# Moving the start addresses of matmul operands in on-chip memory: pads in three pools, wider MLP activation buffers, a smaller reserved scratch

## The chip, the cores and the metric

The kernel runs on one core of one Trainium2 chip. The metric is the device time of one execution in microseconds (us); the median of several runs counts. A core has five engines that work side by side and meet at semaphores: TensorE (PE) multiplies matrices, with its weight loads shown apart as PEld; VectorE (DVE) and ScalarE (ACT) do elementwise work and read PE's results out of PSUM, its accumulator memory; GpSimd (POOL) helps; SyncE (SP) issues most of the DMA transfers. All operands lie in SBUF, the on-chip memory, which has 128 partitions; a tile takes the same byte range in every partition, and an address here is a byte offset within a partition.

## The reference, cut to what matters

Two transformer-like blocks over 256 tokens of width 1024, all in float32. First two layers (a convolution mixed with attention, then a gated linear recurrence), each with a squared-ReLU MLP; then a block with two kinds of attention over 256 tokens and 256 context tokens.

```
h = rmsnorm(x, mix_norm[layer]); x = x + mixer(h)
x = x + square(relu(rmsnorm(x, mlp_norm[layer]) @ w_up)) @ w_down    # 1024 -> 4096 -> 1024
...
return second_block(rmsnorm(x, final_norm), ...)
```

Nearly all arithmetic is in products of activations with weight matrices.

## The kernel before, in words

Activations lie with the channel on the partition: a tile `[128, 8, 256]` holds 8 blocks of 128 channels by 256 tokens. A product in float32 accuracy is made from three products of a cheaper kind, on operands cut in a high and a low part of type float32r: `mm3` (lines 344 to 346) issues weights-high by x-high, weights-high by x-low, weights-low by x-high, all into one PSUM bank. One such matmul holds a 128 by 128 weight block (512 bytes in each partition) in the array and moves 256 tokens through (1,024 bytes in each partition). So each of the three has its own weight load, and the moving operand changes each time too. Products that give a value with the token on the partition (`vproj`, `v`) have it the other way round: the activations are held and 512 columns of a weight tile move.

Weights stream in as 243 units of 512 KB. `fetch` (line 289) issues the DMA of a unit into one of four buffers `raw`; `prep` makes `wh` by a copy (line 296, ACT; line 298 on DVE in some) and `wl` by a subtraction (line 299, DVE or POOL), each in a ring of six tiles of 4,096 bytes. `gemm` uses a unit as 8 weight blocks for one output block, `krow` as 8 output blocks for one row block. In `mlp`, an up pair takes two units (48 matmuls on `xsh` and `xsl`, the two parts of the normalised x, into the bank `mm`), and two units of the down product follow (48 matmuls on `mah` and `mal`, the two parts of the squared ReLU, into four banks `acc`), 16 times over. In each `mah` and `mal` tile there are two row blocks, so a matmul moves one half of it. The instruction stream of an engine runs in its order; that order is made when the program is built, by a scheduler that works from estimated durations, so that an added instruction on one engine can change the order on others.

Tile pools give out addresses in the order in which tiles are first asked for, after a block of 16,384 bytes that is reserved for descriptors of DMAs issued by POOL (there are none here). `wp` holds `raw`, `wh`, `wl`; `cp` holds constants, `xsh`, `xsl`, and the context's `hch`, `hcl` (these two later serve as `q8` and `oa`); phase pools (`l0`, `m0`, `l1`, `m1`, `b2`, ...) are stacked behind them and are given back at the end of their phase.

Of the kernel before, what the change touches and what calls it, by code (L numbers as in the profile page):

```python
# [11 lines left out]
F32 = mybir.dt.float32  # L12
F32R = mybir.dt.float32r
# [231 lines left out]
class Kern:  # L245
# [14 lines left out]
    def t(self, pool, shape, tag, dt=F32, bufs=1):  # L260
        self.n += 1
        return pool.tile(list(shape), dt, tag=tag, name=f"{tag}_{self.n}", bufs=bufs)

    def ps(self, tag="mm", cols=512):
        self.n += 1
        return self.psum.tile([128, cols], F32, tag=tag, name=f"{tag}_{self.n}", bufs=4)
# [32 lines left out]
        (nc.vector if lo == "v" else nc.gpsimd).tensor_tensor(wl, r, wh.bitcast(F32), op=ALU.subtract)  # L299

    def ready(self):
        """splits the next unit into its two parts"""
        i = self.u
        name = self.names[i]
        r = self.fetch(name)
        wh = self.t(self.wp, [128, 1024], "wh", F32R, bufs=RING)
        wl = self.t(self.wp, [128, 1024], "wl", F32R, bufs=RING)
        if i == 0:
            for q in range(4):
                for k in (2 * q, 2 * q + 1):  # L310
                    self.split_scaled(self.x[:, k], self.p("mix", k), self.xs[0][:, k], self.xs[1][:, k])
                if q % 2 == 0:
                    c = slice(q * 256, q * 256 + 512)
                    self.prep(r[:, c], wh[:, c], wl[:, c], "a", "v")
        elif i == 1:
            for c in (slice(0, 512), slice(512, 1024)):
                self.prep(r[:, c], wh[:, c], wl[:, c], "a", "v")
        else:
            c = POLICY.get(name, ("av",))
            c = c[self.cnt.get(name, 0) % len(c)]  # L320
            self.prep(r, wh, wl, c[0], c[1])
        self.cnt[name] = self.cnt.get(name, 0) + 1
        self.q.append((name, (wh, wl)))
# [34 lines left out]
        return ps  # L358

    def gfirst(self, name, x, mid=None):  # L360
        """two pairs at the start of a phase, the blocks of x that come last as late as the order allows"""
        ps, ws = [self.ps(), self.ps()], [[], []]
        for a, k0, k1 in ((0, 0, GA), (1, 0, GB), (0, GA, 8), (1, GB, 8)):
            if not ws[a]:
                ws[a] = [self.unit(name) for _ in range(2)]
            for k in range(k0, k1):
                c = slice(k * 128, k * 128 + 128)
                for i, w in enumerate(ws[a]):
                    self.mm3(ps[a][:, i * T:(i + 1) * T], (w[0][:, c], w[1][:, c]), (x[0][:, k], x[1][:, k]),
                             k == 0 and i == 0, k == 7)  # L370
            if k1 == 8 and mid:
                mid()
                mid = None
        return ps
# [45 lines left out]
        return r  # L420

    def across(self, rc, nt=2):
        """the tokens' values, a token a partition, to all partitions, a token a column"""
        ps = self.ps()
        for j in range(nt):
            self.lasts = self.nc.tensor.matmul(ps[:, j * 128:(j + 1) * 128], rc[:, j:j + 1].to_broadcast([128, 128]),
                                               self.ident, start=True, stop=True)
        return ps[:, :nt * 128]
# [12 lines left out]
    def run(self):  # L441
        nc, ctx = self.nc, self.ctx
        V, S, G, PE = nc.vector, nc.scalar, nc.gpsimd, nc.tensor
        self.wp = ctx.enter_context(self.pool("wp"))
        self.cp = ctx.enter_context(self.pool("cp"))
        self.dp = ctx.enter_context(self.pool("dp", bass.MemoryType.DRAM))
        self.psum = ctx.enter_context(self.pool("psp", bass.MemoryType.PSUM))
# [6 lines left out]
        with self.pool("xp") as xp:  # L454
# [6 lines left out]
            G.memset(self.ones, 1.0)  # L461
            self.mhalf = self.t(cp, [128, 4], "mhalf")
            G.memset(self.mhalf, -0.5)
            with self.pool("l0") as lp:
                self.layer0(lp)
            with self.pool("m0") as mp:
# [6 lines left out]
            with self.pool("m1") as mp:  # L473
                self.hc = self.new_h("hc")
                self.ctx_setup(mp)
                self.mlp(mp, 1)
                self.flush()
            with self.pool("b2h") as hp:
                st = self.b2_head(hp)
        with self.pool("b2") as bp:  # L480
# [11 lines left out]
    def layer0(self, lp):  # L492
        nc = self.nc
        V, S, G, PE = nc.vector, nc.scalar, nc.gpsimd, nc.tensor
        x = self.x
# [4 lines left out]
        z = self.t(lp, [128, 4, PADC + T], "z")  # L500
        G.memset(z[:, :, :PADC], 0.0)
        xs = self.xs = self.new_h()
        w = self.unit("gate", 0)
        ps0, ps1 = self.ps("acc"), self.ps("acc")
        gr = self.ps()
# [281 lines left out]
        self.xs = xs  # L787

    def proj_tail(self, acc, name, ins, gname, g0, xs, R2=None, mp=None, sums=(), after=None):
        """the last row blocks of a projection, output by output, with the residual sum behind each bank"""  # L790
        nc = self.nc
        V, S, G = nc.vector, nc.scalar, nc.gpsimd
        x = self.x
# [69 lines left out]
                self.bg += no  # L863

    def softplus(self, after):
        """8 softplus(-lambda), by parts"""
        nc = self.nc
        V, S = nc.vector, nc.scalar
        sm = self.t(self.cp, [128, 9, 8], "sm")
# [40 lines left out]
    def mlp(self, mp, l):  # L910
# [9 lines left out]
        def up(p):  # L920
            ps = first[p] if p < 2 else self.gpair(("up", "up"), xs)
            r = self.t(mp, [128, 512], "mr", bufs=2)
            a = self.t(mp, [128, 512], "ma", bufs=2)
            ah = self.t(mp, [128, 512], "mah", F32R, bufs=4)
            al = self.t(mp, [128, 512], "mal", F32R, bufs=4)
            S.activation(r, ps, AF.Relu)  # L926
            S.activation(ah, r, AF.Square)
            G.tensor_tensor(a, r, r, op=ALU.mult)  # L928
# [136 lines left out]
        V.scalar_tensor_tensor(h[1][:, k], t, sh, h[0][:, k].bitcast(F32), op0=ALU.add, op1=ALU.subtract)  # L1065

    def b2_head(self, hp):
        """norm of the block's input: x becomes the first block's output, kept in DRAM until the end"""
        nc = self.nc
        V, S, G, PE = nc.vector, nc.scalar, nc.gpsimd, nc.tensor  # L1070
        x, hc = self.x, self.hc
# [426 lines left out]
```

## Time and profile before

| | us |
|---|---|
| three runs | 853.67, 854.93, 857.74 |
| their median | 854.93 |
| span of the profiled execution (its own time) | 859.5 |
| PE busy in it | 817.3 |
| DVE busy | 612.3 |
| ACT busy | 457.5 |
| POOL busy | 226.1 |

The profiled execution is one run apart from the three. It lies 4.6 us above their median; what stands around its span is not recorded apart. The busy time of PE is that of overlapping instructions: a matmul is shown as busy for 0.28 us while the next one starts 0.12 us after it. The pace of PE is therefore read from the distance of starts, and not from the mean duration of an instruction.

### The profile page before, as it was taken

The page shows a single profiled execution, that of the slowest core. Times are in us where ns is not written, and L with a number is a line of the kernel's source. Part 1 is how long each engine was busy: PE and PEld are TensorE (multiplying, and loading weights), DVE is VectorE, ACT ScalarE, POOL GpSimd, SP SyncE. Part 2 cuts the span into 40 slices and gives each one's busy share as a digit, 9 for nine tenths or more (in the row PEclk, how much of TensorE's full clock was granted, in tenths as well). Part 3 has the DMA queues.
Part 4 walks back from the last instruction along what each step waited for, and adds up shares of the span by engine and source line. Part 5 has one row for each costly group of instructions (what it writes and reads, how often), then busy time and mean ns, then how long its engine had stood idle before and what let it go on. Part 6 is the DMA issues. An engine that isn't in the chain of part 4 may idle for free.

```text
span 859.5 us, 16183 instructions
## 1 busy us (share of the span) xinstructions
PE 817.3 (95%) x6472; PEld 783.3 (91%) x6472; DVE 612.3 (71%) x969; ACT 457.5 (53%) x718; POOL 226.1 (26%) x160
## 2 busy tenths in 40 slices
PE   6988999999999999769999999999999999999996
PEld 6976799999999989769999999999988988889996
DVE  5999878999885488997668554447543786655753
ACT  5456556434355444555756444445535577775432
POOL 4784745101111146550314111111100022220001
PEclk9999899999999998898999999999999999999998
DMA  6764247878887543336574655665343532555531
GB/s 227 264 180 145 74 137 270 281 268 288 301 270 244 177 143 124 98 110 211 190 239 158 199 190 181 191 178 165 107 147 115 180 123 75 150 193 162 186 96 49
DMA packets 41258, 152.30 MB, mean 177 GB/s; under 512 B 4576, under 2 KB 5088, under 8 KB 39008
## 3 DMA queue, kind: packets, MB, share of 16 engines
q1 hardware_dynamic: 40752, 149.19, 53.3%
q10 hardware_dynamic: 432, 2.10, 0.7%
q8 instruction: 50, 0.82, 0.4%
q14 instruction: 24, 0.20, 0.1%
HBM read 149.17 MB, written 2.10 MB: 176 GB/s over the span
## 4 chain that ended last, share of the span: by engine, by line
PE 63%; DVE 23%; issue 6%; DMA 3%; ACT 3%; POOL 1%; SPq 0%; DVEq 0%; POOLq 0%; ACTq 0%
PE mm L344 10%; PE mm L345 10%; PE mm L346 10%; PE acc L345 9%; PE acc L346 8%; PE acc L344 8%; DVE wl L299 4%; DVE mm L553 3%; DMA mw<-in_modw 3%; DVE mdump L854 3%; PE acc L1284 2%; PE acc L1312 2%; PE mm L1321 2%; DVE st L638 1%; ACT wh L296 1%
## 5 line engine op out<-in xcount | busy, mean ns | idle before, releaser
L296 ACT ACTIVATE wh<-raw 128x1024 fp32r<-128x1024 f32 (+1 forms) x233 | 243.3, 1050 | 247.5 <-PE mm L345 103.5
L299 DVE TENSOR_TENSOR wl<-raw,wh 128x1024 fp32r<-128x1024 f32 (+1 forms) x201 | 252.1, 1261 | 138.6 <-ACT wh L296 136.6
L346 PE MATMUL mm<-xsh,wl 128*128 128x256 f32 x992 | 280.9, 283 | 2.3 <-DVE wl L299 1.4
L344 PE MATMUL mm<-xsh,wh 128*128 128x256 f32 x992 | 282.6, 285 | 0.0
L345 PE MATMUL mm<-xsl,wh 128*128 128x256 f32 x992 | 280.8, 283 | 1.6 <-DVE xsl L818 1.6
L344 PEld LDWEIGHTS mm<-xsh,wh 128*128 128x128 f32 x992 | 189.8, 191 | 3.7 <-issue 3.3
L346 PEld LDWEIGHTS mm<-xsh,wl 128*128 128x128 f32 x992 | 189.7, 191 | 2.8 <-DVE wl L299 1.6
L345 PEld LDWEIGHTS mm<-xsl,wh 128*128 128x128 f32 x992 | 189.8, 191 | 2.3 <-DVE xsl L818 1.8
L346 PE MATMUL acc<-mah,wl 128*128 128x256 f32 x512 | 143.0, 279 | 1.0 <-DVE wl L299 1.0
L345 PE MATMUL acc<-mal,wh 128*128 128x256 f32 x512 | 143.0, 279 | 0.4 <-DVE mal L391 0.4
L344 PE MATMUL acc<-mah,wh 128*128 128x256 f32 x512 | 143.3, 280 | 0.0
L299 POOL TENSOR_TENSOR wl<-raw,wh 128x1024 fp32r<-128x1024 f32 x42 | 105.5, 2533 | 71.3 <-ACT wh L296 45.5
L928 POOL TENSOR_TENSOR ma<-mr 128x512 f32<-128x512 f32 x32 | 51.3, 1606 | 253.0 <-ACT mr L926 248.3
L346 PEld LDWEIGHTS acc<-mah,wl 128*128 128x128 f32 x512 | 96.2, 188 | 1.4 <-DVE wl L299 1.4
L345 PEld LDWEIGHTS acc<-mal,wh 128*128 128x128 f32 x512 | 96.3, 188 | 0.6 <-DVE mal L391 0.6
L344 PEld LDWEIGHTS acc<-mah,wh 128*128 128x128 f32 x512 | 96.3, 188 | 0.0
L854 DVE CUSTOM_DVE_ANT_0 mdump<-mw,cv 128x1024 f32<-128x1024 f32 x40 | 50.2, 1256 | 3.8 <-DMA mw<-in_modw 3.6
L345 PE MATMUL acc<-ysl,wh 128*128 128x256 f32 x128 | 38.3, 301 | 7.2 <-DVE ysl L391 7.2
L553 DVE SCALAR_TENSOR_TENSOR mm<-z,cwh,mm 128x256 f32<-128x256 f32 x106 | 44.6, 476 | 0.2
L1303 POOL TENSOR_SCALAR P<-P,st 128x512 f32<-128x512 f32 x32 | 22.3, 698 | 84.2 <-DVE st L1302 57.0
L391 DVE TENSOR_TENSOR mal<-ma,mah 128x512 fp32r<-128x512 f32 x32 | 22.8, 714 | 16.8 <-POOL ma L928 16.8
L345 PEld LDWEIGHTS acc<-ysl,wh 128*128 128x128 f32 x128 | 26.2, 205 | 8.0 <-DVE ysl L391 7.6
(346 smaller groups left out, 1364.8 us busy)
## 6 DMA issues: line engine op xcount, KB each, us to landing
raw<-in_wst SPq DMA_DIRECT2D x240, 512.0 KB, 3.7
mw<-in_modw SPq DMA_DIRECT2D x12, 1024.0 KB, 7.2
nb<-in_nab SPq DMA_DIRECT2D x16, 256.0 KB, 3.6
ab<-in_alibi ACTq DMA_DIRECT2D x1, 1536.0 KB, 9.5
x<-in_xT SPq DMA_DIRECT2D x4, 256.0 KB, 4.4
cv<-in_cvec SPq DMA_DIRECT2D x1, 1024.0 KB, 4.8
cx<-in_cT SPq DMA_DIRECT2D x1, 1024.0 KB, 4.8
xd<-x SPq DMA_DIRECT2D x1, 1024.0 KB, 4.5
```

What stands on the lines that cost most here:

```text
L296: nc.scalar.activation(wh, r, AF.Copy)
L299: (nc.vector if lo == "v" else nc.gpsimd).tensor_tensor(wl, r, wh.bitcast(F32), op=ALU.subtract)
L344: mm(out, w[0], x[0], start=start, stop=False, skip_group_check=True)
L345: mm(out, w[0], x[1], start=False, stop=False, skip_group_check=True)
L346: return mm(out, w[1], x[0], start=False, stop=stop, skip_group_check=True)
L391: self.nc.vector.tensor_tensor(l, src, h.bitcast(F32), op=ALU.subtract)
L553: return V.scalar_tensor_tensor(conv[:, j] if i == 30 else ca, zs, c, ca, op0=ALU.mult, op1=ALU.add)
L854: V.tensor_tensor_reduce(d, w, cv[:, s * 1024:(s + 1) * 1024], 0.5, 0.0, op0=ALU.mult, op1=ALU.add, accum_out=self.mod[:, s * 24 + i:s * 2 ...
L928: G.tensor_tensor(a, r, r, op=ALU.mult)
L1284: PE.matmul(sc[i], Q[tag, h][a][:, qs], K[tag, h][b], start=a + b == 0, stop=a == 1)
L1303: G.tensor_scalar(P, P, st[:, 3:4], 0.0, op0=ALU.mult, op1=ALU.add)
L1312: PE.transpose(pt[:, i * 128:(i + 1) * 128], P[:, i * 128:(i + 1) * 128], self.ident)
```

## The change

It makes no change in what is computed. Tiles get other start addresses, by five edits, and four tiles that nobody reads are filled with zeros by POOL:

1. The reserved block shrinks from 16,384 to 1,024 bytes.
2. A pad of 384 bytes stands ahead of `raw`, one of 352 bytes ahead of `xsh`, one of 256 bytes behind `xsl`, one of 128 bytes behind `hcl`, each a tile with a MEMSET on POOL.
3. `mah` and `mal` tiles are 2,112 bytes long in place of 2,048; the first 2,048 are used.

Some comments at the head of functions are dropped as well, and line numbers grow by 6 to 10.

```diff
+    def pad(self, pool, nbytes):
+        self.n += 1
+        t = pool.tile([128, nbytes // 4], F32, tag=f"pad{self.n}", name=f"pad_{self.n}", bufs=1)
+        self.nc.gpsimd.memset(t, 0.0)
...
         self.wp = ctx.enter_context(self.pool("wp"))
+        self.pad(self.wp, 384)
...
             G.memset(self.mhalf, -0.5)
+            self.pad(cp, 352)
             with self.pool("l0") as lp:
...
                 self.mlp(mp, 1)
                 self.flush()
+            self.pad(cp, 128)
             with self.pool("b2h") as hp:
...
         xs = self.xs = self.new_h()
+        self.pad(self.cp, 256)
         w = self.unit("gate", 0)
...
-            ah = self.t(mp, [128, 512], "mah", F32R, bufs=4)
-            al = self.t(mp, [128, 512], "mal", F32R, bufs=4)
+            ah = self.t(mp, [128, 528], "mah", F32R, bufs=4)[:, :512]
+            al = self.t(mp, [128, 528], "mal", F32R, bufs=4)[:, :512]
...
-    nc = _bacc.Bacc("TRN2", target_bir_lowering=False, num_devices=1)
+    nc = _bacc.Bacc("TRN2", target_bir_lowering=False, num_devices=1, dynamic_dma_scratch_size=1024)
```

Where the operands of the float32r matmuls start, as the remainder of the address by 512 bytes (a weight block or a row block inside a tile lies a multiple of 512 bytes further on):

| tiles | before | after |
|---|---|---|
| `raw`, `wh`, `wl` | 128 | 0 |
| `xsh`, `xsl` | 288 | 0 |
| `hch`, `hcl` (also `oa`) | 32 | 0 |
| `mah`, four buffers | 416 each | 0, 64, 128, 192 |
| `mal`, four buffers | 416 each | 256, 320, 384, 448 |
| `ysh`, `ysl` of layer 0 | 480 | 64 |
| layer 1: `ysh` (in the place `xr`), `ysl` | 416, 0 | 0, 96 |
| layer 1: `xch`, `xcl` | 0 | 96 |
| second block: `kb`, `vb`, `ob`, `ckh`, `ckl`, `wkh`, `wkl`, `kh`, `kl`, `qh`, `ql`, `cqh`, `cql` | 416 | 0 |

The order on the engines is the same but for the pads and some ten places in layer 0. Three of them follow.

POOL at the start of the program, before: the constants `mhalf`, the two averaging matrices `on`, the zero border of `z`, then the squares of x (`ss`) and their sum.

```order
L463 MEMSET mhalf_84 128x4
L497 MEMSET on_9_89 128x128
L499 MEMSET on_10_91 128x128
L501 MEMSET z_93 128x4x30
L509 TENSOR_TENSOR ss_20_129<-x_74 128x512
L509 TENSOR_TENSOR ss_21_130<-x_74 128x512
L510 TENSOR_TENSOR ss_20_129<-ss_20_129,ss_21_130 128x512
```

And with the change, at the same place:

```order
L470 MEMSET mhalf_86 128x4
L268 MEMSET pad_88 128x88
L506 MEMSET on_11_93 128x128
L508 MEMSET on_12_95 128x128
L510 MEMSET z_97 128x4x30
L268 MEMSET pad_101 128x64
L519 TENSOR_TENSOR ss_23_135<-x_76 128x512
L519 TENSOR_TENSOR ss_24_136<-x_76 128x512
L268 MEMSET pad_6910 128x32
L520 TENSOR_TENSOR ss_23_135<-ss_23_135,ss_24_136 128x512
```

Two pads stand among the constants, the last one between the squares and their sum (the first of the four, of 96 columns, stands ahead of all this).

ACT in layer 0, before: the copies `wh` of weight units, and the half tanh (`gv`) of the fourth gate of the convolution.

```order
L296 ACTIVATE wh_503<-raw_501 128x1024
L296 ACTIVATE wh_537<-raw_535 128x1024
L558 ACTIVATE gv_448<-gv_448 128x256
L296 ACTIVATE wh_567<-raw_565 128x1024
L296 ACTIVATE wh_627<-raw_625 128x1024
```

With the change:

```order
L302 ACTIVATE wh_509<-raw_507 128x1024
L302 ACTIVATE wh_543<-raw_541 128x1024
L302 ACTIVATE wh_573<-raw_571 128x1024
L568 ACTIVATE gv_454<-gv_454 128x256
L302 ACTIVATE wh_633<-raw_631 128x1024
```

One copy of a weight unit (`wh_567` before, `wh_573` now) now stands ahead of that tanh.

DVE at the end of the convolution, before: the partial sums of the POOL taps are added (line 731), the last two taps make `conv` (line 553), then the variance (line 414) reads what PE summed, and `lsq` (line 754) adds two channel blocks for the next sum on PE.

```order
L731 TENSOR_TENSOR mm_229<-mm_229,ss_70_469 128x256
L731 TENSOR_TENSOR mm_310<-mm_310,ss_70_469 128x256
L553 SCALAR_TENSOR_TENSOR conv_195<-z_93,cwh_189,mm_229 128x256
L553 SCALAR_TENSOR_TENSOR conv_195<-z_93,cwh_189,mm_310 128x256
L414 TENSOR_SCALAR var_1195<-mm_1190 128x2
L754 TENSOR_TENSOR lsq_1083<-conv_195 128x256
```

With the change:

```order
L741 TENSOR_TENSOR mm_235<-mm_235,ss_73_475 128x256
L563 SCALAR_TENSOR_TENSOR mm_316<-z_97,cwh_195,mm_316 128x256
L563 SCALAR_TENSOR_TENSOR conv_201<-z_97,cwh_195,mm_235 128x256
L741 TENSOR_TENSOR mm_316<-mm_316,ss_73_475 128x256
L420 TENSOR_SCALAR var_1201<-mm_1196 128x2
L563 SCALAR_TENSOR_TENSOR conv_201<-z_97,cwh_195,mm_316 128x256
L764 TENSOR_TENSOR lsq_1089<-conv_201 128x256
```

The variance, which reads a result of PE, now stands ahead of the last tap.

## Rows read from the trace of the kernel before

**Rows 1.** The page of the profile: busy time by engine, and the TensorE clock granted in 40 equal slices of the span (a digit is tenths of full speed).

```profile
PE 817.3 (95%) x6472; PEld 783.3 (91%) x6472; DVE 612.3 (71%) x969; ACT 457.5 (53%) x718; POOL 226.1 (26%) x160
...
PEclk9999899999999998898999999999999999999998
```

**Rows 2.** Busy time of each engine in stretches of the span: the start and end of the stretch and its length, busy us and instructions (x) of PE, PEld, DVE, ACT and POOL, the granted clock, the busy share of the DMA engines, GB/s. The first three lie in layer 0, the next two in its MLP, the last in the MLP of layer 1.

```profile
30.00:60.00 30.00, 26.93 (x223) 25.51 (x221) 30.00 (x68) 14.02 (x24) 22.32 (x10) 0.97 0.71 232
60.00:85.00 25.00, 22.29 (x124) 18.46 (x123) 24.79 (x76) 17.21 (x47) 14.18 (x6) 0.90 0.39 125
85.00:120.00 35.00, 31.67 (x223) 28.37 (x222) 28.62 (x62) 20.04 (x41) 22.59 (x17) 0.90 0.29 94
120.00:210.00 90.00, 89.58 (x758) 89.38 (x757) 84.27 (x126) 45.74 (x59) 22.85 (x14) 1.00 0.78 267
210.00:305.00 95.00, 92.60 (x784) 92.01 (x783) 66.03 (x80) 45.96 (x54) 15.00 (x9) 1.00 0.74 243
425.00:600.00 175.00, 175.00 (x1485) 175.00 (x1484) 102.69 (x109) 92.20 (x117) 31.14 (x21) 1.00 0.59 186
```

**Rows 3.** The page: shares of the span on the chain that ended last, by engine.

```profile
PE 63%; DVE 23%; issue 6%; DMA 3%; ACT 3%; POOL 1%; SPq 0%; DVEq 0%; POOLq 0%; ACTq 0%
```

**Rows 4.** Groups of PE matmuls by line and operands: the result, the two operands (moving first for products with weights), columns, count, busy us, mean ns, idle us before them and who ended it.

```profile
L344 PE MATMUL mm<-xsh,wh 128*128 128x256 f32 x992 | 282.6, 285 | 0.0
L344 PE MATMUL acc<-xsh,wh 128*128 128x256 f32 x64 | 19.0, 297 | 0.0
L344 PE MATMUL acc<-mah,wh 128*128 128x256 f32 x512 | 143.3, 280 | 0.0
L345 PE MATMUL mm<-hcl,wh 128*128 128x256 f32 x80 | 22.5, 281 | 0.0
L345 PE MATMUL acc<-ysl,wh 128*128 128x256 f32 x128 | 38.3, 301 | 7.2 <-DVE ysl L391 7.2
L344 PE MATMUL acc<-wh,xsh 128*128 128x512 f32 x32 | 13.6, 426 | 2.7 <-DVE st L636 2.7
L344 PE MATMUL acc<-wh,hch 128*128 128x512 f32 x16 | 6.3, 392 | 0.0
```

**Rows 5.** PE in order of time, MLP of layer 1: the first matmul of an up pair, of the down pair that follows, and of the next up pair; 48 matmuls start from one row to the next. The first column is the start in us.

```profile
516.28 0.28 PE L344 MATMUL mm<-xsh,wh 128*128 128x256 f32 x1
...
522.03 0.28 PE L344 MATMUL acc<-mah,wh 128*128 128x256 f32 x1
...
527.64 0.28 PE L344 MATMUL mm<-xsh,wh 128*128 128x256 f32 x1
```

**Rows 6.** The same in the MLP of layer 0; again 48 from one row to the next.

```profile
265.65 0.28 PE L344 MATMUL mm<-xsh,wh 128*128 128x256 f32 x1
...
271.35 0.28 PE L344 MATMUL acc<-mah,wh 128*128 128x256 f32 x1
...
276.95 0.28 PE L344 MATMUL mm<-xsh,wh 128*128 128x256 f32 x1
```

**Rows 7.** PE in order of time, second block: the first product on `xsh` and the last of the run; 143 matmuls lie from one row to the other.

```profile
614.47 0.28 PE L344 MATMUL mm<-xsh,wh 128*128 128x256 f32 x1
...
631.25 0.28 PE L346 MATMUL mm<-xsh,wl 128*128 128x256 f32 x1
```

**Rows 8.** PE in order of time, output projection of layer 0; 8 matmuls lie from one row to the other.

```profile
124.08 0.28 PE L344 MATMUL acc<-ysh,wh 128*128 128x256 f32 x1
...
125.04 0.28 PE L346 MATMUL acc<-ysh,wl 128*128 128x256 f32 x1
```

**Rows 9.** PE in order of time, layer 1, in a stretch that was granted half the clock; one matmul a row.

```profile
357.03 0.41 PE L344 MATMUL acc<-xch,wh 128*128 128x256 f32 x1
357.24 0.41 PE L345 MATMUL acc<-xcl,wh 128*128 128x256 f32 x1
357.45 0.41 PE L346 MATMUL acc<-xch,wl 128*128 128x256 f32 x1
```

**Rows 10.** The same operands some us later at the full clock; 9 matmuls lie from the first row to the last.

```profile
363.36 0.28 PE L345 MATMUL acc<-xcl,wh 128*128 128x256 f32 x1
...
364.43 0.28 PE L346 MATMUL acc<-xch,wl 128*128 128x256 f32 x1
```

**Rows 11.** PE in order of time, matmuls of 512 columns: 9 lie from the first row to the second; the three on `ckh` and `ckl` are ended by the transpose in the last row.

```profile
647.86 0.39 PE L344 MATMUL acc<-wh,hch 128*128 128x512 f32 x1
...
649.96 0.39 PE L344 MATMUL acc<-wh,xsh 128*128 128x512 f32 x1
...
698.02 0.39 PE L344 MATMUL mm<-ckh,wkh 128*128 128x512 f32 x1
...
698.71 0.49 PE L1312 MATMUL acc<-ident,P 128*128 128x128 f32 x3
```

**Rows 12.** POOL in order of time at the start (start, length; in brackets the idle time before and what ended it).

```profile
1.55 0.20 POOL L499 MEMSET on<- 128x128 f32 x1
1.70 0.20 POOL L501 MEMSET z<- 128x120 f32 x1
6.46 2.49 POOL L509 TENSOR_TENSOR ss<-x 128x512 f32<-128x512 f32 x2 [4.56 <-DMA x<-in_xT]
9.02 1.34 POOL L510 TENSOR_TENSOR ss<-ss,ss 128x512 f32<-128x512 f32 x1
```

**Rows 13.** ACT and DVE in order of time around the fourth gate of the convolution.

```profile
40.80 0.42 ACT L558 ACTIVATE gv<-gv 128x256 f32<-128x256 f32 x1 [1.33 <-DVE gv L557]
41.58 1.06 ACT L296 ACTIVATE wh<-raw 128x1024 fp32r<-128x1024 f32 x1 [0.35 <-DMA raw<-in_wst]
...
44.16 1.28 DVE L562 SCALAR_TENSOR_TENSOR z<-gv 128x256 f32<-128x256 f32 x1
```

**Rows 14.** DVE in order of time at the end of the convolution.

```profile
98.28 0.86 DVE L553 SCALAR_TENSOR_TENSOR conv<-z,cwh,mm 128x256 f32<-128x256 f32 x2
99.68 0.16 DVE L414 TENSOR_SCALAR var<-mm 128x2 f32<-128x2 f32 x1 [0.54 <-PE mm L408]
99.76 2.60 DVE L754 TENSOR_TENSOR lsq<-conv 128x256 f32<-128x256 f32 x1
```

## The prediction, made before the change was run

> **What bounds the kernel now.** Read first the page's busy times [rows 1]: PE is busy for 95% of the span. The chain that ended last runs on PE for 63% and on DVE for 23% [rows 3]; where that is which, the stretches tell [rows 2]. From 425 to 600 us, in the MLP of layer 1, PE is busy for 175.00 of 175.00 us while DVE has 102.69; from 120 to 305 it has all but 2.8 us. So in both MLPs, in the projections and in the second block the end is set by how fast PE starts its matmuls, and a nanosecond gained on each is gained in full. Only 30 to 120 us are different: DVE is busy for 30.00 of 30 us, then 24.79 of 25, PE has idle time, and a faster PE only waits longer.
>
> The pace of PE comes next: 175.00 us over 1,485 matmuls [rows 2] is 117.8 ns from start to start. At half the clock the same kind starts every 0.21 us [rows 9], by these rounded rows 205 to 215 ns; the level nearest to 256 columns at 1.2 GHz is 213, and half of that, 106.7 ns, is what a matmul would take at 2.4 GHz if the array never stood still. Each therefore loses some 11 ns, about 9%. This loss is all the change can touch.
>
> The loss isn't the same everywhere, and that is the main observation. The two halves of one MLP, with the same weights, engines and DMA beside them, have two paces. In layer 1, 48 matmuls on `xsh`, `xsl` take 5.75 us, or 119.8 ns each, and the 48 on `mah`, `mal` right behind them 5.61, or 116.9 [rows 5]. In layer 0 it is 5.70 (118.8) against 5.60 (116.7) [rows 6]. In the second block 143 on `xsh`, `xsl` take 16.78 us, or 117.3 [rows 7]; eight on `ysh`, `ysl` 0.96, or 120 [rows 8]; nine on `xch`, `xcl` 1.07, or 118.9 [rows 10]. By where the moving operand starts (the weights start at 128 throughout): 416 has 116.7 to 116.9; 288 has 117.3 to 119.8, in my average 118.6, the middle of [rows 5, 7]; 480 has 120; 0 has 118.9. The paces of one operand thus come in levels, and which of them it gets isn't settled by its address alone.
>
> **What the change adds.** The pads' MEMSETs: three stand ahead of the squares on POOL, which had been idle for 4.56 us waiting for x [rows 12]; a MEMSET of 128 columns takes 0.20 us there and starts 0.15 after its neighbour, so three smaller ones (under 0.6 us) are hidden by that idle time. Without that cover they would cost 0.5. The fourth stands between the squares and their sum: at most 0.1 us. ACT's copy ahead of the fourth half tanh takes 1.06 us [rows 13] and its input came at 41.58, so the tanh moves from 40.80 to some 42.7; its user on DVE starts `z` at 44.16, so it stays hidden by 1 us. On DVE the variance, which waited 0.54 us for PE, now stands ahead of the last tap, so that tap (half of 0.86 us) no longer fills the wait, and `lsq` behind it comes up to 0.4 us later [rows 14]; PE's next sums wait for `lsq`. Together +0.5 us; between 0 and +1.0, since DVE sets the end there. A smaller scratch costs nothing: nothing is issued from it.
>
> **What it moves.** [Rows 4] give the counts; a group on one part stands for its three products.
>
> First, `xsh`, `xsl` from 288 and `hch`, `hcl` from 32 to 0, with the weights from 128 to 0: (992 + 64) × 3 = 3,168 and 80 × 3 = 240, together 3,408, of which I take 3,260 as running back to back at full clock (the others lie in 30 to 120 us or at half clock). They now have 118.6 ns. No row shows operands that both start at 0. The nearest in kind is `ckh` times `wkh`, where both start at the same remainder, 416: three matmuls of 512 columns take 0.69 us, 230 each, against 2.10 for nine, 233.3, with `wh` moving from 128 [rows 11]. That is 1.4% less; 1.4% off 118.6 is 116.9, and the lowest levels seen are 116.7 and 117.3. I take 117.0, halfway: 3,260 × 1.6 ns = −5.2 us. The bounds for this term within the levels seen: all at 116.7, −6.2; at 120, +4.6.
>
> Second, `mah`, `mal`, 512 × 3 = 1,536 matmuls [rows 4], from 416, the best start of the trace, to eight starts 64 apart. Equal shares of the four starts seen (116.8, 118.6, 120, 118.9) would mean 118.6, so +2.7 us; if the weights' start matters and not theirs, they keep 116.8, so 0. I take a little under the middle, +1.1, since the weights change for all of them.
>
> Third, `ysh`, `ysl` of layer 0 (128 × 3 on both layers by [rows 4], half of them here; 7.2 us of idle time belong to this group) from 480 to 64: 192 × (120 − 118.6) = −0.3. Layer 1's `ysh`, `ysl`, `xch`, `xcl` are few and go from one class to another: 0 within ±0.3.
>
> Fourth, the matmuls of 512 columns, (32 + 16) × 3 = 144 [rows 4], with `wh` moving from 0 in place of 128: 3.3 ns each at the most by [rows 11], 0.5 us; I take half, −0.3. The second block's tiles that go from 416 to 0 keep their distance from the weights of their own kind or are few: 0.
>
> The sum: −5.2 + 1.1 − 0.3 − 0.3 + 0.5 = −4.2 us. The profiled execution took 859.5 us in its span, 4.6 more than the median 854.93; a difference of pace carries over, so **850.7 us**, −0.5%. With the first term at its best (−6.2) and the second at 0 it is 848.6; with all at 117.3 (−4.2), the second at +2.7 and the order on DVE at +1.0, 853.8. That is the main case's own range.
>
> **The rivals.** *A new, lower level.* Before, weights start at 128 everywhere but in the few products of the second block, so a 512-byte weight block always lies over two stretches of 512 bytes, and in most matmuls 1,024 moving bytes lie over three. If a loss is paid for each moving stretch begun, 10.0 ns for three, then two cost 6.7, and the pace becomes 113.3: 3,260 × 5.3 = −17.3 us, and −1.5 for some 430 matmuls that go from 416 to 0; with +0.5 it is 837. For it: the matmul of 512 columns on `ckh`, over five stretches, loses 230 − 213.3 = 16.7, five times 3.3. Against it: `xch`, `xcl` start at 0 and have 118.9 [rows 10], and `wh` moving over five loses 20 [rows 11]. Its far end, the loss gone entirely on the xs operands, would be 3,260 × 11.9 = −39, near 816.
>
> By the Trainium skill, "TensorE: Matmul & The Clock Gate", section "Wait — 56ns, not 53.3ns?", a warm matmul starts every N ÷ 2.4 GHz plus about 2.5 ns, which for 256 columns would be an estimated 109.2 ns; the trace here nowhere shows that in a sustained run [rows 5 to 8], its best being 116.7, so the page's figure is what a matmul without the loss would have and doesn't say what takes the rest.
>
> *Addresses don't set the pace.* The two paces in one MLP could come from what went before (how DVE, ACT and the weight loads fell against PE at the start of a run), since 288 alone shows 117.3 and 119.8 [rows 5, 7]. Then the change does nothing that can be told: 855.4 with the +0.5, and with levels dealt anew ±4. Against it: 416 has 116.7 to 116.9 in both MLPs.
>
> All starts before and after are multiples of 32 bytes. The Trainium skill, "SBUF — State Buffer", section "Door 1: The DMA port swizzle (why `[64,N]` ≈ `[32,N]`)", knows 16-byte lines in SBUF, crossed at a cost; by that rule each operand here crosses as many lines as before, and the time would be that of this rival.
>
> *Slower: the upper level.* `mah`, `mal` leave the one start with a steady 116.8, and the xs operands, now at the same remainder as the weights that are loaded beside them, could lock into the highest level seen, 120 [rows 8]. Price: 1,536 × 3.2 = +4.9 and 3,260 × 1.4 = +4.6, with +0.5 it is **864.9**. It decides once the mean pace of all some 5,500 matmuls rises by 0.8 ns (4.3 us). For it: 0 as a start shows 118.9, not the low level, and a common start could as well mean that two readers meet at one place. Against it: `ckh` times `wkh`, the only pair with a common start, is the fastest of its kind [rows 11].
>
> **How the numbers follow.** The main case has 0.40, split about evenly by 850.7, which is 0.5% below the median; 0.5%, or 4.3 us, is about what a measurement of this kernel can tell from no change. The lower level has 0.20 (0.03 of it at the far end). No effect has 0.20: 0.03 of it falls below, 0.15 within, 0.02 above. The slower case has 0.20, all but 0.02 of it above 859.2. Faster: 0.21 + 0.20 + 0.03 = 0.44. Slower: 0.18 + 0.02 = 0.20. Same: 0.36. The range reaches down to the middle of the lower level, 837, and up short of the slower case's price, 862, so that about 0.2 is left out: half of the lower level and half of the slower case.
>
> **What the profile would show.** In both MLPs, divide the distance of the first starts of neighbouring up and down groups by 48, as in [rows 5, 6]: the main case has up groups near 117.0, down groups at 116.8 to 118.6; the lower level has up groups near 113.3; no effect has 116.7 to 120 as before; the slower case 120 in both. The 512-column products should go from 233.3 to 230. On POOL the squares still begin when x arrives; around the fourth gate `z` keeps its place; at the end of the convolution `lsq` starts up to 0.4 us later. Should the slices with a lower clock [rows 1] lie elsewhere or last longer, the sum is off by what they take, and that has nothing to do with addresses. The prediction is wrong if up groups with operands at 0 keep more than 118.6 ns, or if a level below 116.7 appears.

## The result: slower by half a per cent, and the profile after

The changed kernel takes 860.35 us, the median of seven runs (858.64 to 863.33), against 855.13 of before (853.67 to 857.92): a ratio of 1.0056, 95% interval 1.0035 to 1.0077, or 3.0 to 6.6 us more. The forecast was 850.7.

The two profiled executions hide this: their spans are 859.5 and 860.2 us. The views of the cores give the reason. Before (first row) ran at a mean granted clock of 0.975 in its profiled execution, which is less than the change had (second row):

```profile
core 0: 859.5 us, clock 0.975
...
core 0: 860.2 us, clock 0.979
```

A clock of 0.979 against 0.975 is 0.4% of 860 us, or some 3 us of PE at full speed; it differs from execution to execution of one kernel (0.977 to 0.983 in the seven of the change). So the pace in stretches of full clock must be compared, not the spans. Nor may a span be set against a run's time: the profiled execution of the change took 862.52 us as a run, 2.3 more than its span, so the one of before lay further above its median than 4.6 us. The page of the change first: busy time, clock by slices, shares of the chain that ended last.

```profile
PE 821.5 (96%) x6472; PEld 787.4 (92%) x6472; DVE 609.7 (71%) x969; ACT 457.1 (53%) x718; POOL 225.9 (26%) x164
...
PEclk9998899999999999899999999999999999999998
...
PE 67%; DVE 20%; issue 7%; ACT 2%; POOL 2%; DMA 1%; SPq 0%; DVEq 0%; POOLq 0%; ACTq 0%
```

PE holds 67% of the chain, where it had 63 [rows 3]; all busy times are equal to within some 0.5% [rows 1]. The same stretches as in [rows 2], two in layer 0 and one in the MLP of layer 1:

```profile
120.00:210.00 90.00, 89.74 (x756) 89.54 (x755) 83.95 (x125) 46.10 (x59) 23.90 (x14) 1.00 0.77 265
210.00:305.00 95.00, 94.05 (x791) 93.63 (x790) 66.65 (x80) 45.23 (x53) 14.02 (x9) 1.00 0.73 245
425.00:600.00 175.00, 175.00 (x1479) 175.00 (x1478) 101.80 (x110) 90.55 (x115) 31.27 (x21) 1.00 0.61 188
```

In the last, PE is busy throughout as before, but starts 1,479 matmuls where it started 1,485. Where that is lost shows in PE's order of time: the first matmul of each up and each down group in that MLP, 48 starts from one row to the next, as in [rows 5].

```profile
520.88 0.28 PE L350 MATMUL acc<-mah,wh 128*128 128x256 f32 x1
...
526.64 0.28 PE L350 MATMUL mm<-xsh,wh 128*128 128x256 f32 x1
...
532.40 0.29 PE L350 MATMUL acc<-mah,wh 128*128 128x256 f32 x1
...
537.86 0.28 PE L350 MATMUL mm<-xsh,wh 128*128 128x256 f32 x1
...
543.60 0.28 PE L350 MATMUL acc<-mah,wh 128*128 128x256 f32 x1
...
549.30 0.28 PE L350 MATMUL mm<-xsh,wh 128*128 128x256 f32 x1
...
555.05 0.28 PE L350 MATMUL acc<-mah,wh 128*128 128x256 f32 x1
...
560.71 0.29 PE L350 MATMUL mm<-xsh,wh 128*128 128x256 f32 x1
```

Divide the distances by 48. The four down groups have 5.76, 5.46, 5.70 and 5.66 us, or 120.0, 113.8, 118.8 and 117.9 ns a matmul. They use the four buffers in turn, whose starts lie 0, 192, 128 and 64 bytes past a multiple of 256. The up groups between them, all on operands that start at a multiple of 256, have 5.76, 5.74 and 5.75, or 120.0, 119.6 and 119.8. In the second block 143 matmuls on `xsh`, `xsl` take 17.16 us, exactly 120.0, where they had 117.3 [rows 7]:

```profile
613.77 0.28 PE L350 MATMUL mm<-xsh,wh 128*128 128x256 f32 x1
...
630.93 0.28 PE L352 MATMUL mm<-xsh,wl 128*128 128x256 f32 x1
```

The matmuls of 512 columns went the other way, 2.04 us for nine, or 226.7, from 233.3 [rows 11]:

```profile
646.52 0.39 PE L350 MATMUL acc<-wh,hch 128*128 128x512 f32 x1
...
648.56 0.39 PE L350 MATMUL acc<-wh,hch 128*128 128x512 f32 x1
```

Three of the fills stand among the constants of POOL, ahead of its wait of 4.90 us for x, and one between squares and sum, 0.12 us long [rows 12]. Around the fourth gate the tanh starts at 41.42 us, 0.6 later than before, but `z` at 42.11, 2 us earlier [rows 13]. At the end of the convolution the variance waits 0.82 us for PE and the last tap follows it [rows 14]; `lsq` starts 1.3 us later than before, since PE's sum comes 0.7 later and the tap takes 0.6. The first experiment tells whether any of this costs time.

```profile
2.06 0.15 POOL L268 MEMSET pad<- 128x64 f32 x1
7.11 2.22 POOL L519 TENSOR_TENSOR ss<-x 128x512 f32<-128x512 f32 x2 [4.90 <-DMA x<-in_xT]
9.27 0.12 POOL L268 MEMSET pad<- 128x32 f32 x1
```

```profile
100.40 0.16 DVE L420 TENSOR_SCALAR var<-mm 128x2 f32<-128x2 f32 x1 [0.82 <-PE mm L414]
100.47 0.47 DVE L563 SCALAR_TENSOR_TENSOR conv<-z,cwh,mm 128x256 f32<-128x256 f32 x1
101.05 2.05 DVE L764 TENSOR_TENSOR lsq<-conv 128x256 f32<-128x256 f32 x1
```

Taken over all back to back matmuls of 256 columns at full clock (start to start, from the trace, breaks left out), the mean pace is 117.97 ns before and 119.06 after. 1.09 ns on 5,500 matmuls is 6 us; the 512-column ones give 0.8 back. That lies within the 3.0 to 6.6 us measured.

### The profile page after: what moved, and what is told of

It reads as the page before. It is cut to its first block, busy times and chain, and to the rows that moved or that the text cites. A ratio compares the mean times of both kernels' runs of the same rounds, so it can differ in the third digit from the quotient of the medians.

```text
span 860.2 us, 16187 instructions
## 1 busy us (share of the span) xinstructions
PE 821.5 (96%) x6472; PEld 787.4 (92%) x6472; DVE 609.7 (71%) x969; ACT 457.1 (53%) x718; POOL 225.9 (26%) x164
## 4 chain that ended last, share of the span: by engine, by line
PE 67%; DVE 20%; issue 7%; ACT 2%; POOL 2%; DMA 1%; SPq 0%; DVEq 0%; POOLq 0%; ACTq 0%
PE mm L350 11%; PE mm L352 10%; PE mm L351 10%; PE acc L351 9%; PE acc L350 9%; PE acc L352 9%; DVE wl L305 4%; DVE mdump L864 3%; DVE mm L563 2%; PE acc L1294 2%; PE acc L1322 2%; PE mm L1331 2%; DVE st L648 1%; DMA mw<-in_modw 1%; ACT wh L302 1%
```

## The experiments

**Theory:** the pace of a matmul depends on where its moving operand starts relative to the weights, by the remainder by 256 bytes (called the distance below). **Rivals:** the moving operand's own start; fills and order; chance at the start of a run.

**The same addresses.** All that the change adds, without the moves.

```diff
-        self.pad(self.wp, 384)   # the others 352, 256, 128
+        self.pad(self.wp, 512)   # all four 512
-            ah = self.t(mp, [128, 528], "mah", F32R, bufs=4)[:, :512]   # al likewise
+            ah = self.t(mp, [128, 512], "mah", F32R, bufs=4)[:, :512]
```

> The change with pads of 512 bytes and MLP activation buffers 2,048 bytes apart, so that every operand starts at the remainder by 512 that it had before; the fills, the order on the engines and the small scratch stay. Theory (addresses alone cost the 5 us): the time of before, 855 us, ratio 1.000, up groups of the MLPs at 117 to 120 ns a matmul as before, down groups at 116.7. Rival (fills and the new order cost it): 860 us, ratio 1.006, with the paces of before.

Ratio 0.9999 (0.9977 to 1.0021), and the old paces are back: an up group of 5.76 us (120.0) and a down group of 5.60 (116.7), and 118.7 and 116.8 as means over the MLPs and the second block, as before.

```profile
519.43 0.28 PE L350 MATMUL mm<-xsh,wh 128*128 128x256 f32 x1
...
525.19 0.28 PE L350 MATMUL acc<-mah,wh 128*128 128x256 f32 x1
...
530.79 0.28 PE L350 MATMUL mm<-xsh,wh 128*128 128x256 f32 x1
```

So fills, order and scratch cost nothing that can be told; the addresses cost the 5 us.

**The moving operands of the norms, the MLPs and the second block 192 past the weights**, where one buffer of the change had 113.8.

```diff
-            self.pad(cp, 352)
+            self.pad(cp, 544)
-            ah = self.t(mp, [128, 528], "mah", F32R, bufs=4)[:, :512]   # al likewise
+            ah = self.t(mp, [128, 512], "mah", F32R, bufs=4)[:, :512]
```

> The pad ahead of xsh is 192 bytes longer and the MLP buffers are 2,048 bytes apart, so that xsh, xsl, hch, hcl, mah, mal, kb, vb, ob and cq start 192 bytes past a multiple of 256, with weights at 0. Theory (the start of the moving operand, by the remainder by 256 and perhaps counted from the weights' start, sets the pace): 113.7 ns in place of 119.9 on 3,260 matmuls (-20 us), 113.7 in place of 117.6 on 1,536 (-6 us), -2 us on some 340 of the second block, +0.4 us on ysh and ysl of layer 0, which come to 256: 832 us, ratio to before 0.973. Rival (levels are dealt by how a run starts, not by addresses): 855 to 861 us, ratio 1.00, with levels of 116.7 to 120 in both MLPs.

842.64 us, ratio 0.9862 (0.9829 to 0.9895). Up and down groups of this stretch take 5.44 us each, 113.3 ns:

```profile
505.61 0.28 PE L350 MATMUL mm<-xsh,wh 128*128 128x256 f32 x1
...
511.05 0.28 PE L350 MATMUL acc<-mah,wh 128*128 128x256 f32 x1
...
516.49 0.28 PE L350 MATMUL mm<-xsh,wh 128*128 128x256 f32 x1
```

The direction is as expected, the size was not: 832 was expected. Two reasons show. About one group in five runs at 117.8, at the same addresses (of which more below), so that the operands that were moved have 114.3 in the mean and not 113.7, some 3 us. And PE, idle for 38.7 us of the span in the change, is idle for 45.4 here (from 210 to 305 us it is busy for only 92.33, where the change had 94.05): part of what PE gains is spent waiting.

**Weights and moving operands moved together** by 64 bytes; the distance stays 192, but the moving operands start at a multiple of 256.

```diff
-        self.pad(self.wp, 384)
+        self.pad(self.wp, 448)   # on top of the edit before
```

> The same with a pad 64 bytes longer ahead of the weights, which moves weights and moving operands together by 64 bytes: weights at 64, moving operands at 256, their distance still 192. Distance theory (what counts is the moving start less the weights' start, by the remainder by 256): 113.7 ns and 832 us as in all_192. Start theory (the moving operand's own address counts): a start at a multiple of 256 has 120 ns, 3,260 x 6.2 + 1,536 x 6.2 more than all_192, 862 us.

Ratio 0.9878 (0.9843 to 0.9914), groups of 5.44 us again:

```profile
516.02 0.28 PE L350 MATMUL mm<-xsh,wh 128*128 128x256 f32 x1
...
521.46 0.28 PE L350 MATMUL acc<-mah,wh 128*128 128x256 f32 x1
```

A start at a multiple of 256 has 120.0 with weights beside it at a multiple of 256, and 113.3 with weights 64 further on. The moving operand's own start falls as an explanation; the distance stands.

**The weights alone**: moving operands at their old starts, weights at 0.

```diff
-            self.pad(cp, 352)   # behind it 256 and 128
+            self.pad(cp, 128)   # behind it 512 and 512
-            ah = self.t(mp, [128, 528], "mah", F32R, bufs=4)[:, :512]   # al likewise
+            ah = self.t(mp, [128, 512], "mah", F32R, bufs=4)[:, :512]
```

> One part of the change alone: the weights start at 0, every moving operand at the remainder that it had before (pads elsewhere make up for the 384 bytes), buffers of the MLP 2,048 bytes apart, fills, order and scratch as in the change. Distances by 256 become 32 for xsh, xsl, hch, hcl (before 160) and 160 for mah, mal (before 32). Theory (the distance sets which levels there are): up groups at 116.7 to 117.8 in place of 117.2 to 120, 3,260 x 1.6 ns = -5.2 us; down groups at 117.4 in place of 116.8, +0.9 us; ysh, ysl -0.3; together -4.6 us, ratio to before 0.995. Rival (the start of the moving operand alone): the paces of before, ratio 1.000. Rival (weight blocks that lie in one piece of 512 bytes cost more, or less, by themselves): both groups move the same way.

Ratio 1.0003 (0.9982 to 1.0024), and under it the two groups have exchanged their paces: the up group has 5.61 us (116.9), the down group 5.75 (119.8), the reverse of [rows 5], by a move of the weights alone.

```profile
523.17 0.28 PE L350 MATMUL mm<-xsh,wh 128*128 128x256 f32 x1
...
528.78 0.28 PE L350 MATMUL acc<-mah,wh 128*128 128x256 f32 x1
...
534.53 0.28 PE L350 MATMUL mm<-xsh,wh 128*128 128x256 f32 x1
```

As means 116.8 (3,260 matmuls, from 118.6) and 119.0 (1,536, from 116.8), and `kb`, `vb`, `ob` near 119.4 from 116.7: −5.7 + 3.3 + 0.9 = −1.5 us, at the edge of what the ratio allows (−1.5 to +2.1). My expected gain of 4.6 had taken 117.4 for distance 160 from a single run; before's own `xsh`, with 118.6 there, was the better row. The single levels change hands as well: steady groups at distance 32 have 116.7 or 117.8, and at 160 117.3, 118.7 or 120.0, on `mah` and `xsh` before, on `xsh` and `mah` here.

**One part undone**: buffers 2,048 bytes apart, so that all eight start at distance 0.

```diff
-            ah = self.t(mp, [128, 528], "mah", F32R, bufs=4)[:, :512]   # al likewise
+            ah = self.t(mp, [128, 512], "mah", F32R, bufs=4)[:, :512]
```

> The change with one part undone: MLP activation buffers 2,048 bytes apart again, so that all eight start at a multiple of 256 as the weights do. Theory (distance 0 costs 120 ns a matmul): down groups of both MLPs at 120.0 in place of 119.9, 118.0, 118.7 and 113.7 by buffer, 1,536 x 2.4 ns = +3.6 us against the change, ratio to before 1.010. Rival (the spacing of 2,112 bytes is what costs, the down groups were at 116.8 before): -1 us against the change, ratio 1.004.

Down groups at 120.0, all of them; 862.22 us, ratio 1.0066 (1.0042 to 1.0090). The pace is as the theory has it; against the change's 1.0056 the 3.6 us can't be told, since the intervals overlap, though both lie above 1. By the paces, the wider spacing is the part of the change that limits the damage.

**A map of the distance.** Rings of eight buffers, one start each, in the changed kernel, one line for each of three kernels (`al` likewise):

```diff
-            ah = self.t(mp, [128, 528], "mah", F32R, bufs=4)[:, :512]   # al likewise
+            ah = self.t(mp, [128, 520], "mah", F32R, bufs=8)[:, :512]     # multiples of 32
+            ah = self.t(mp, [128, 520], "mah", F32R, bufs=8)[:, 4:516]    # 16 bytes on
+            ah = self.t(mp, [128, 584], "mah", F32R, bufs=8)[:, s:s + 512]  # s by buffer: starts 176 to 216
```

> The change with a ring of eight mah and eight mal buffers 2,080 bytes apart, so that their starts stand at 0, 32, 64 ... 224 past a multiple of 256, each in a down group of 48 matmuls four times in all, with weights at 0. Distance theory: 120 at 0, 116.8 at 32, 117.7 at 64, 118 to 120 at 96, 118.6 at 128 and 160, 113.7 at 192, and 224 unknown. Start theory, from before where weights stood at 128: 118.6 at 32, 116.8 at 160, 119.9 at 224. Rival without addresses: no order among the eight. Time about 858 us.

> The ring of eight mah and mal buffers again, each used from 16 bytes past its start, so that the starts stand at 16, 48, 80 ... 240 past a multiple of 256, weights at 0. If the pace is a smooth function of the distance with one dip at 192, then 176 and 208 lie between 113.7 and their neighbours (117.4 at 160, 118.4 at 224), near 115.5; if only multiples of 64 bytes matter (64-byte pieces of a read meeting), 176 reads as 160 or 192 does and 208 as 192 or 224.

> The ring of eight with starts at 176, 184, 188, 192, 196, 200, 208 and 216 past a multiple of 256, weights at 0. A smooth dip: 113.3 within some bytes of 192, rising on both sides. A step: one pace on one side of 192 up to it and another from 196 on, or 113.3 from 192 as far as the next step. If a start better than 192 exists it shows here as a pace under 113.3 ns.

A single run each: 857.27, 860.59 and 860.0 us. Mean ns from start to start, four groups of 48 for each distance (176, 192 and 208 come in two of the kernels):

```
distance   0    16    32    48    64    80    96   112   128   144   160
ns       119.9 117.8 117.3 118.4 117.9 119.8 119.3 116.4 119.0 118.5 117.4
distance 176   184   188   192   196   200   208   216   224   240
ns       119.4 120.1 119.8 113.7 121.1 120.0 119.4 120.6 118.4 117.2
```

No smooth dip, no step: among these groups 192 alone has 113.7 every time, and 4 bytes beside it the pace is among the worst. Some of the means hide two levels: at 32 two groups have 116.7 and two 117.9, at 112 two 114.9 and two 117.9, at 196 two 122.1 and two 120.1. Of the third kernel, the down groups at 188, 192 and 196 (first, third and fifth row): 5.76, 5.46 and 5.77 us.

```profile
540.64 0.28 PE L350 MATMUL acc<-mah,wh 128*128 128x256 f32 x1
...
546.40 0.28 PE L350 MATMUL mm<-xsh,wh 128*128 128x256 f32 x1
...
552.15 0.29 PE L350 MATMUL acc<-mah,wh 128*128 128x256 f32 x1
...
557.61 0.28 PE L350 MATMUL mm<-xsh,wh 128*128 128x256 f32 x1
...
563.35 0.29 PE L350 MATMUL acc<-mah,wh 128*128 128x256 f32 x1
...
569.12 0.29 PE L350 MATMUL mm<-xsh,wh 128*128 128x256 f32 x1
```

Nor does 113.3 belong to distance 192 alone. In `ring8`, the output projection of layer 0, where `ysh` and `ysl` start at distance 64 as in the change, has 64 matmuls in 7.26 us, 113.4 each:

```profile
114.27 0.28 PE L352 MATMUL acc<-ysh,wl 128*128 128x256 f32 x1
...
121.53 0.28 PE L350 MATMUL mm<-xsh,wh 128*128 128x256 f32 x1
```

The same 64 at the same addresses take 7.54 us in the change (from 118.59), 117.8 each, both times behind a wait of 1.07 us for DVE's `ysl`. In `ring8_fine` 25 others of this projection have 113.3. So 64 has the two levels of 192, and it was dealt the upper one in most runs.

**Whose distance: of the weights held, or of those being loaded?** With the MLP buffers 2,048 bytes apart, a pad behind `wh` moves `wl` to 192 and, as in `all_192`, the moving operands:

```diff
-        wl = self.t(self.wp, [128, 1024], "wl", F32R, bufs=RING)
+        i or self.pad(self.wp, 192); wl = self.t(self.wp, [128, 1024], "wl", F32R, bufs=RING)
```

> all_192 with a pad of 192 bytes between the ring of wh and that of wl (and 192 bytes less ahead of xsh): moving operands and wl start at 192, wh at 0. Of the three products of a weight block, the first two (wh) have distance 192 from the weights that are held, the third (wl) distance 0. Theory A (the weights held while the operand moves count): 113.5, 113.5 and 120 ns to the next start. Theory B (the weights that are loaded meanwhile for the next matmul count): the first, followed by wh, 113.5; the second, followed by wl, 120; the third, followed by the next block's wh, 113.5. Rival (distance to wh alone, or addresses past 64 bytes, don't matter): 113.5 for all three. Under A and B the mean is 115.7 and the time some 846 us.

Neither. On `xsh`, `xsl` the three products have 118.4, 118.7 and 117.5 ns, and most groups run at 117.8 throughout, also behind the short matmuls that bring 113.3 in the kernels with one distance (below). Two distances in one sequence don't average; the sequence has a pace of its own. (The 869.29 us of its single run are not a matter of pace alone: in layer 0 one `z` step on DVE takes 13.09 us, 2.00 in the change, and PE waits 11.1 us for what follows it. Why is not known.)

**Different distances for the two parts**, weights at 0:

```diff
-            ah = self.t(mp, [128, 528], "mah", F32R, bufs=4)[:, :512]
+            ah = self.t(mp, [128, 584], "mah", F32R, bufs=8)[:, h:h + 512]   # al with l; h, l by buffer
```

> The change with a ring of eight buffers whose mah and mal start at different distances from the weights (mah, mal): 192, 192; 192, 0; 192, 64; 192, 128; 0, 192; 64, 192; 128, 192; 64, 0. If each matmul has the pace of its own distance, the 48 of a group average two parts mah to one part mal: for 192, 0 (2 x 113.4 + 120) / 3 = 115.6, for 0, 192 (2 x 120 + 113.4) / 3 = 117.8, for 192, 64 some 114.9. If one pace holds for the whole group and is set by how all three steps follow each other, the groups with two different distances have levels of their own, not these means, and 192, 192 alone keeps 113.3.

A single run, 856.21 us; mean ns from start to start by pair:

```
mah, mal  192,192  192,0  192,64  192,128  0,192  64,192  128,192  64,0
ns         113.7   117.8  117.9    118.7   117.8  117.9    119.8   119.0
```

Where 115.6 was expected for 192, 0 there are 117.8, the same as for 0, 192. So a pace belongs to a sequence of starts, and of these eight only the one with 192 at every step has the low one.

**The last operands as well.** In `all_192`, `ysh`, `ysl`, `xch`, `xcl` still had other distances.

```diff
-        ys = (self.t(lp, [128, 8, T], "ysh", F32R), self.t(lp, [128, 8, T], "ysl", F32R))
+        ys = (self.t(lp, [128, 8 * T + 48], "ysh", F32R)[:, 48:].rearrange("p (a b) -> p a b", a=8),
+              self.t(lp, [128, 8, T], "ysl", F32R))
-        xr = self.t(lp, [128, 8, 3 + T], "xr")
+        xr = self.t(lp, [128, 8 * (3 + T) + 40], "xr")[:, :8 * (3 + T)].rearrange("p (a b) -> p a b", a=8)
```

> all_192 with ysh, ysl of both layers and xch, xcl at distance 192 from the weights as well (wider tiles in place of more pads, so the order of all engines is that of all_192). Before this, in all_192, 3 x 57 matmuls of layer 0 run at 119.7 ns and 3 x 57 of layer 1 at 123, 117 and 120. Theory (levels of distance 192 are 113.3 and 117.8): 340 matmuls x 2 to 6 ns = -1 to -2 us against all_192, ratio to before 0.984, if none of this lies behind a wait for DVE. Rival (a group whose start is dealt the upper level gains nothing): the time of all_192, ratio 0.986.

844.56 us, ratio 0.9835 (0.9819 to 0.9851): faster than both kernels, and not to be told from `all_192`.

**What picks the level.** In it, from 448 us on, the pace in the MLP of layer 1 changes at two places, while no distance does. The short matmuls on `ones` stand at the first, the transposing ones on `ident` at the second:

```profile
469.58 0.50 PE L414 MATMUL mm<-ones,ssum 128*128 128x1 f32 x4
...
475.67 0.28 PE L350 MATMUL mm<-xsh,wh 128*128 128x256 f32 x1
...
481.33 0.28 PE L350 MATMUL acc<-mah,wh 128*128 128x256 f32 x1
...
492.63 0.61 PE L432 MATMUL mm<-ident,rv 128*128 128x128 f32 x4
...
498.53 0.28 PE L350 MATMUL mm<-xsh,wh 128*128 128x256 f32 x1
...
503.97 0.28 PE L350 MATMUL acc<-mah,wh 128*128 128x256 f32 x1
```

Between them a group takes 5.66 us (117.9), behind the second 5.44 (113.3). So the second was moved:

```diff
-            if p == 8:
+            if p == 7:
                 R2 = self.spread(mp, rv, "R2")
```

> all_192_ys with the broadcast of the MLP's root mean square (two transposing matmuls on ident and rv) issued one pair earlier, p == 7 in place of p == 8. In all_192_ys the pace in the MLP of layer 1 goes from 113.3 to 117.8 ns at the four short matmuls on ones and ssum (469.6 us) and back at those on ident and rv (492.6). Theory (a matmul of another kind between two runs shifts how the reads of moving operand and weights fall against each other, and that, with the distance, picks the level until the next such break): the stretch at 117.8 after ones and ssum ends at the new place of ident and rv, 96 matmuls or some 11 us earlier, and the time falls by 96 x 4.4 ns = 0.4 us a layer, which can't be told: ratio 0.983. Rival (the level changes by what DVE, ACT or the transfers do there): the pace goes back to 113.3 where it did before, or at another place than the moved matmuls.

```profile
465.14 0.50 PE L414 MATMUL mm<-ones,ssum 128*128 128x1 f32 x4
...
476.89 0.61 PE L432 MATMUL mm<-ident,rv 128*128 128x128 f32 x4
...
482.79 0.28 PE L350 MATMUL mm<-xsh,wh 128*128 128x256 f32 x1
...
488.23 0.28 PE L350 MATMUL acc<-mah,wh 128*128 128x256 f32 x1
```

The fast pace now begins 11.8 us after `ones`, where it had been 23.1: with the moved matmuls, at once. (843.62 us, 0.9852, 0.9820 to 0.9883: no difference in time, as expected.) A wait can do the same without any matmul of another kind. In the MLP of layer 0 of `all_192_ys`, 48 matmuls take 5.44 us (113.3), then PE waits 0.38 us for `wl`, and the next 45 take 5.30 (117.8):

```profile
193.63 0.28 PE L350 MATMUL mm<-xsh,wh 128*128 128x256 f32 x1
...
199.07 0.28 PE L350 MATMUL acc<-mah,wh 128*128 128x256 f32 x1
...
199.83 0.38 PE L352 MATMUL acc<-mah,wl 128*128 128x256 f32 x1 [0.38 <-DVE wl L305]
200.06 0.28 PE L350 MATMUL acc<-mah,wh 128*128 128x256 f32 x1
...
205.36 0.28 PE L350 MATMUL mm<-xsh,wh 128*128 128x256 f32 x1
```

The distance sets which levels there are; how a run begins, behind a matmul of another kind or a wait, picks one, and it holds until the next such break.

## Why the prediction was wrong

The bound was read rightly: PE's start to start pace sets the end in the MLPs and the second block, and fills, order and the smaller scratch cost nothing that shows (0.5 us was allowed). The terms, in the order of the prediction, with the mean paces that were measured:

| term | forecast | measured |
|---|---|---|
| `xsh`, `xsl`, `hch`, `hcl`, 3,260 matmuls | 118.6 to 117.0, −5.2 us | 118.57 to 119.83, +4.1 us |
| `mah`, `mal`, 1,536 | +1.1 | 116.82 to 117.52, +1.1 |
| `ysh`, `ysl` of layer 0, 192 | −0.3 | 119.7 to 117.7, −0.4 |
| 512 columns, 144 | −0.3 | 233.6 to 227.7, −0.8 |
| `kb`, `vb`, `ob`, `cqh`, `cql`, some 340 | 0 | 116.7 to 119.9, +1.1 |
| order on DVE, fills | +0.5 | within −2.0 and +1.8 |

The measured terms add up to +5.1 us, the ratio says +4.8.

**The step that failed** is the first term. It took the pace of operands with a common start from `ckh` times `wkh`, because they were the only pair with one [rows 11]. That row was a bad neighbour twice. It has three matmuls, 0.69 us read to 0.01. And it is of 512 columns, and these do not follow the map of the 256-column ones: `wh` moving at distance 0 has 226.7 and is the fastest of its kind in the change, while 256 columns at distance 0 have 120.0 and are near the slowest. The table of paces in the prediction held the moving operand's start, with the weights at 128; with the weights' start subtracted it would have read 32: 116.8, 160: 118.6, 96: 120, 128: 118.9. Those are distances, and the runs confirm them as such for 32 and 128 within 0.6 ns; none of them was 0, so the trace held no row of 256 columns for it, and both ends of the range should have weighed alike. Both signs of being wrong that the prediction named came: up groups at 120.0, and a level below 116.7, the 113.7 of one buffer. That the time lies inside the stated range of 837 to 862 is owed to the range's width: the forecast was a gain.

The second line is right by luck: three of the four starts lie 1.1 to 3.1 ns above the old 116.8, and the fourth, at 113.7, lies below every level that was priced.

The fifth line failed by the same error: "keep their distance from the weights of their own kind" was right for the attention's tiles, but `kb`, `vb`, `ob` and `cq` are used with `wh`, from distance 32 to 0.

**The rival that won** is the slower one, by what it said of the xs operands: a lock into the upper level, 120, at a common start (+4.6 priced, +4.1 measured). Its reason, that two readers meet at one place, isn't shown, and a common start isn't needed: distances 80, 184 and 200 have 119.8 to 120.1 too. Its other half, `mah` and `mal` at 120 in all buffers for +4.9, did not come: the four starts have 119.9, 117.9, 118.5 and 113.7, so 860.35 and not 864.9. Its point of decision, a rise of the mean pace by 0.8 ns, was passed with 1.09.

**No effect of addresses** was half right. Addresses set the levels (`same_addresses`, `all_192`), but at one distance a run can have one of two or three, and what broke the stream before it decides (`spread_p7`). By the 16-byte lines of the Trainium skill ("SBUF — State Buffer", section "Door 1: The DMA port swizzle (why `[64,N]` ≈ `[32,N]`)") nothing would change here; the trace disagrees, with 120.0 at distance 0 and 113.7 at 192, both multiples of 16.

**The lower level**, 113.3, exists, but not for the reason given there, and that its number came out is luck: the operands that begin fewest stretches of 512 bytes, at distance 0, have 120, and 113.3 was seen at distances 192 and 64 alone. Nothing came below it. The Trainium skill ("TensorE: Matmul & The Clock Gate", section "Wait — 56ns, not 53.3ns?") has some 2.5 ns over the columns' own time; the least in any sustained run here is 113.3 − 106.7 = 6.6 ns, so on these operands that figure was not reached.

**What stays open:** why 192 and 64, and why 4 bytes beside 192 the level is gone; why a sequence of two distances has a pace of its own; which level a wait or a short matmul will pick. That the reads of moving operand and weights hinder each other would fit (only their distance counts), but no view of the profile shows such a stall, and a run without weight loads beside the matmuls wasn't tried.

## What to carry to other kernels

Where PE is busy without a gap, read its pace from start to start, group by group, beside the addresses of both operands: 113.3 to 120 ns for the same matmul is 6%, and no busy time shows it. Round addresses are no virtue in themselves; here a common remainder of weights and moving operand was near the worst, and one offset, read off a ring of buffers with a start each, gave 1.4 to 1.6%. Before taking a price from the nearest row, check that the row is of the same shape and ask which variable it really shows.

## What was not expected of the hardware

- The pace of float32r matmuls of 256 columns, each with its own weights, depends on the distance of moving operand and weights by the remainder by 256 bytes: 113.3 ns at 192, 119.8 at 188, 121.1 at 196, 120.0 at 0. Moving both by 64 bytes leaves the levels (113.3).
- One distance can have several levels: 113.3 and 117.8 at 192 and at 64, 116.7 and 117.8 at 32, 117.3, 118.7 and 120.0 at 160; at 0 nearly all groups have 120.0. A few short matmuls of another kind, or a wait of 0.38 us, switch between them.
- Matmuls of 512 columns follow another order: 226.7 at distance 0, 233.3 at 96.
